# An encoder layer on one core: the seventh of eight input pairs by Strassen's products, weights split four blocks at a time, one pool of 8 KB raw tiles, and a first sum made by an adding DMA

## The chip, the core and the metric

The kernel runs on one core of a Trainium2 chip. The metric is the device time of one execution in microseconds (us). The core's engines are TensorE (PE, matrix products), VectorE (DVE), ScalarE (ACT), GpSimd (POOL) and SyncE (SP, which here only issues DMAs). They run side by side, each through its own queue in order, and wait for each other by semaphores.

## The reference

One layer of an encoder for 256 positions of 2048 channels, in float32: a feed-forward half-step, a mixer, and another feed-forward half-step.

```python
def _swiglu(x, w_gate, w_up, w_down):
    return (jax.nn.silu(x @ w_gate) * (x @ w_up)) @ w_down

def _macaron_ffn(x, pre_g, w_gate, w_up, w_down, post_g):
    return x + MACARON_WEIGHT * _rms_norm(_swiglu(_rms_norm(x, pre_g), w_gate, w_up, w_down), post_g)
...
    for l in range(DEPTH):
        h = _macaron_ffn(h, ffn1_pre_g[l], ffn1_w_gate[l], ffn1_w_up[l], ffn1_w_down[l], ffn1_post_g[l])
        h = _gated_mixers(h, mix_pre_g[l], w_in[l], b_gate[l], q_norm_g[l], k_norm_g[l],
                          w_attn_o[l], w_fourier[l], w_out[l], mix_post_g[l], rope)
        h = _macaron_ffn(h, ffn2_pre_g[l], ffn2_w_gate[l], ffn2_w_up[l], ffn2_w_down[l], ffn2_post_g[l])
```

The mixer is an attention branch (16 query heads, 4 key and value heads) and a Fourier branch, each behind a sigmoid gate. The hidden width of the feed-forward is 5632.

## The kernel before

**Products in pieces.** TensorE gets float32r operands. `split` (L104) cuts a float32 weight tile into a rounded part `hi` (ACT, L105) and the rest `lo` (DVE, L106), and `mm3` (L109) makes one product with three matmuls of 128x128 by 128x512 (L111, L112, L113): hi by hi, hi by lo, lo by hi. A block of weights below is 128 rows of 512 columns, 256 KB in DRAM, 2 KB in each partition. Every weight is read once from DRAM into a raw tile, split, and multiplied with both halves of the 256 positions.

**The feed-forward.** `ffn` (L714) works in 11 blocks of 512 hidden columns. The first two are multiplied plainly, column block by column block. For the nine others (f = 2 to 10) the products of the gate and up weights are made by `swiglu` (L562), and between them stand the products with the down weights, `row_line` (L666), two blocks behind. The 2048 input channels are eight pairs of 128-channel blocks. For six pairs (`BY_SEVEN`: 0, 1, 2, 4, 5, 6) the two halves of the positions, the two blocks of channels and the two weights (gate, up) make a 2x2 product of 2x2 blocks, done by Strassen's seven products instead of eight (`seven`, L606): 21 matmuls instead of 24. Pairs 3 and 7 are done plainly (`plain`, L576). The sums of the input that the seven products need are made once by `Forms` (L447) and kept split; the sums of the weights are made by DVE for each block of columns (`minus`, L586: four differences of one block of weights per pair), and so are the sums of the products at the end, with SiLU and the last multiplication (L591, L599, L603).

**The order of the work.** In this stage the order on DVE, ACT and PE is written out by hand (`manual_schedule`): each engine runs its instructions in the order of the program. The other queues (SP's and POOL's DMAs) are ordered by a scheduler. `Line` (L529) holds a queue of steps. A step has a part that makes weights ready (load, differences, split) and a part that uses them (matmuls, then sums or copies). `feed` (L535) puts a step in; while the queue is full it first runs `next`, which puts out the use of the oldest step; then it puts out the preparation of the new one. So DVE and ACT prepare up to eight steps ahead of the matmuls. `hold` on a step stops preparations after its use until a step without it has been used, so that sums of products stand ahead of further splits on DVE. A step holds two blocks of weights: two steps for each column block of `row_line`, four for a pair of seven products, the last with one block.

**Rooms.** Split tiles come from a ring: six pairs of 4 KB tiles, and two more 8 KB tiles out of `b8`, twelve rooms of 8 KB that also hold u (the input, split and transposed), the forms, y, h and other large tiles. Raw tiles come from five rooms of 4 KB, and for pairs 0, 2, 4 and 6 from `b8`, with one load of 1024 KB. `chunk` has three rooms of each of its two kinds. A room is given again when its last reader is done: a load waits for the split that read the room before, a split for the matmuls.

**The rows.** In `row_line` the first result is set into y. Later the first two column blocks are added to y by an adding DMA on POOL's queue (L706), the other two by copying y into PSUM ahead of the products (L690) and back (L700).

**Mixer.** It runs plain column blocks (`col_block`) and row blocks with two-block pieces of weights from the same rooms; `gate` (L1103) writes its sigmoids into `b8` rooms mB and zA; the fold of the Fourier branch adds by DMA while it loads (`load_f`, L934). `last_rows` (L265) ends each stage and starts the next.

## Time and profile before

| | |
|---|---|
| three timed runs | 1998.6, 1999.6 and 2001.35 us, median 1999.6 |
| the profiled execution | 2000.01 us, its span from the first to the last instruction 1997.9 us |
| granted TensorE clock | 0.998 |
| DMA | 434.19 MB, 217 GB/s on the mean |
| the span by engines | PE 99% busy, DVE 89%, ACT 65%, POOL 4% |

The shares of busy time and the chain that ended last are on the profile's page. A row of the windows gives, for a stretch of the span, the busy time and number of instructions of PE, PE's weight loads (PEld), DVE, ACT and POOL, then the granted clock, the share of the DMA engines and GB/s. A row of the groups by form gives the line, engine, operation, tiles and shapes, the number, then total busy time and mean ns of one, and behind the second bar the idle time ahead of them with what ended it. A row of the timeline gives start, duration and instruction. A row of the DMA issues gives the tile and source, the issuing queue, the number, the size of each, and the median us from issue to landing. The waits give who waited for whom: total us, times, longest.

### The profile page before, as it was taken

What the parts mean: (1) busy time and instruction counts of PE and PEld (TensorE: products, weight loads), DVE (VectorE), ACT (ScalarE), POOL (GpSimd) and SP (SyncE); (2) the same over time, 40 slices, a digit from 0 to 9 for tenths busy, and PEclk for the clock granted to TensorE, in tenths of its full rate; (3) what the DMA queues carried; (4) which work ended last, traced back from release to release, by engine and by line L of the source; (5) the groups of instructions that cost most, each with busy time, mean ns of one, the idle gap of its engine ahead of it and who ended that gap; (6) DMA issues with size and microseconds to landing.
All of it is one profiled execution on the core that took longest, in us unless ns stands there. A gap on an engine that the chain in (4) does not pass through costs nothing.

```text
span 1997.9 us, 25756 instructions
## 1 busy us (share of the span) xinstructions
PE 1983.4 (99%) x9146; PEld 1644.7 (82%) x9146; DVE 1776.0 (89%) x2306; ACT 1301.3 (65%) x1860; POOL 84.8 (4%) x94
## 2 busy tenths in 40 slices
PE   9999999999999999999999999999999999999998
PEld 7888888888888888888888888888888888888886
DVE  6999999999999878886877885878999999999996
ACT  7566766767666756556666564656667766677666
POOL 0000000000000010100000000000000000000002
PEclk9999999999999999999999999999999999999999
DMA  9657766677668796854555557565577766677673
GB/s 328 222 177 237 227 221 204 207 242 224 227 203 277 241 302 202 252 181 142 192 193 186 193 166 276 195 216 194 177 230 232 232 209 208 216 232 232 215 259 127
DMA packets 117584, 434.19 MB, mean 217 GB/s; under 512 B 12840, under 2 KB 18992, under 8 KB 106064
## 3 DMA queue, kind: packets, MB, share of 16 engines
q1 hardware_dynamic: 103888, 411.65, 60.4%
q0 software_dynamic: 13568, 20.91, 6.0%
q8 instruction: 71, 1.16, 0.2%
q14 instruction: 57, 0.47, 0.1%
HBM read 409.44 MB, written 6.29 MB: 208 GB/s over the span
## 4 chain that ended last, share of the span: by engine, by line
PE 98%; DVE 1%; DMA 1%; ACT 0%; issue 0%; SPq 0%; DVEq 0%; ACTq 0%
PE pc L112 20%; PE pc L111 20%; PE pc L113 20%; PE pr L113 11%; PE pr L112 11%; PE pr L111 11%; PE pt L184 2%; PE pe L111 0%; PE pe L113 0%; PE pf L112 0%; PE pf L111 0%; PE pf L113 0%; DVE wlo L106 0%; PE pe L112 0%; PE pt L1081 0%; DMA raw<-in_f_gate 0%
## 5 line engine op out<-in xcount | busy, mean ns | idle before, releaser
L106 DVE TENSOR_TENSOR wlo<-raw,whi 128x1024 fp32r<-128x1024 f32 (+1 forms) x567 | 680.7, 1219 | 96.2 <-ACT whi L105 94.1
L105 ACT ACTIVATE whi<-raw 128x1024 fp32r<-128x1024 f32 (+1 forms) x567 | 586.5, 1053 | 252.3 <-PE pc L113 96.1
L112 PE MATMUL pc<-wlo,fh 128*128 128x512 f32 x738 | 287.6, 390 | 0.0
L113 PE MATMUL pc<-whi,fl 128*128 128x512 f32 x738 | 287.6, 390 | 0.0
L111 PE MATMUL pc<-whi,fh 128*128 128x512 f32 x738 | 287.4, 389 | 0.0
L111 PE MATMUL pc<-whi,uh 128*128 128x512 f32 x688 | 271.6, 396 | 1.2 <-ACT uh L838 1.2
L113 PE MATMUL pc<-whi,ul 128*128 128x512 f32 x688 | 269.7, 392 | 0.0
L112 PE MATMUL pc<-wlo,uh 128*128 128x512 f32 x688 | 269.3, 392 | 0.1
L105 ACT ACTIVATE whi<-t 128x1024 fp32r<-128x1024 f32 (+1 forms) x198 | 171.5, 866 | 138.6 <-DVE t L586 133.6
L586 DVE TENSOR_TENSOR t<-raw 128x512 f32<-128x512 f32 (+1 forms) x252 | 208.9, 841 | 14.2 <-DMA raw<-in_f_gu 10.5
L111 PE MATMUL pr<-whi,hTh 128*128 128x512 f32 x544 | 213.6, 393 | 0.0
L113 PE MATMUL pr<-whi,hTl 128*128 128x512 f32 x544 | 212.0, 390 | 0.0
L112 PE MATMUL pr<-wlo,hTh 128*128 128x512 f32 x544 | 211.9, 390 | 0.0
L106 DVE TENSOR_TENSOR wlo<-t,whi 128x1024 fp32r<-128x1024 f32 (+1 forms) x198 | 193.4, 977 | 13.6 <-ACT whi L105 13.3
L105 ACT ACTIVATE w<-raw 128x1024 fp32r<-128x1024 f32 x144 | 151.9, 1055 | 40.4 <-DVE raw L586 35.2
L106 DVE TENSOR_TENSOR w<-raw,w 128x1024 fp32r<-128x1024 f32 x144 | 175.5, 1219 | 0.0
L112 PEld LDWEIGHTS pc<-wlo,fh 128*128 128x128 f32 x738 | 138.6, 188 | 29.1
L111 PEld LDWEIGHTS pc<-whi,fh 128*128 128x128 f32 x738 | 138.6, 188 | 29.0
L113 PEld LDWEIGHTS pc<-whi,fl 128*128 128x128 f32 x738 | 138.6, 188 | 28.8
L111 PEld LDWEIGHTS pc<-whi,uh 128*128 128x128 f32 x688 | 129.7, 188 | 27.9 <-ACT uh L838 2.7
L112 PEld LDWEIGHTS pc<-wlo,uh 128*128 128x128 f32 x688 | 129.6, 189 | 26.8 <-DVE wlo L106 1.7
L113 PEld LDWEIGHTS pc<-whi,ul 128*128 128x128 f32 x688 | 129.4, 188 | 27.0
(350 smaller groups left out, 3183.4 us busy)
## 6 DMA issues: line engine op xcount, KB each, us to landing
raw<-in_f_down SPq DMA_DIRECT2D x176, 512.0 KB, 5.2
raw<-in_f_gu SPq DMA_DIRECT2D x144, 512.0 KB, 4.5
raw<-in_f_gu SPq DMA_DIRECT2D x72, 1024.0 KB, 7.4
raw<-in_w_in SPq DMA_DIRECT2D x112, 512.0 KB, 4.4
raw<-in_f_up SPq DMA_DIRECT2D x32, 512.0 KB, 5.0
raw<-in_w_ao SPq DMA_DIRECT2D x32, 512.0 KB, 3.8
raw<-in_w_out SPq DMA_DIRECT2D x32, 512.0 KB, 4.9
raw<-in_f_gate SPq DMA_DIRECT2D x31, 512.0 KB, 5.8
```

The lines of the kernel that those rows point to most:

```text
L105: a = A.activation(hi, src, AF.Copy)
L106: v = V.tensor_tensor(out=lo, in0=src, in1=hi.bitcast(F32), op=ALU.subtract)
L111: T.matmul(ps, lh, rh, start=first, stop=False, skip_group_check=onto)
L112: T.matmul(ps, lh, rl, start=False, stop=False, skip_group_check=onto)
L113: return T.matmul(ps, ll, rh, start=False, stop=last, skip_group_check=onto)
L184: T.transpose(pt[:, j, :], src[:, j * P:(j + 1) * P], ident[:])
L586: V.tensor_tensor(out=out, in0=a, in1=b, op=ALU.subtract)
```

## The change

Seven pairs go through Strassen's products (`BY_SEVEN` is 0 to 6), and only pair 7 is plain. The seven products are formed in another way: a pair's four raw blocks are split at once and give four products (p1, g0, p5, u0); then three sums of blocks are split at once and give three (p6, p7, g1). The first sum is already in the raw tile: one block is loaded, the three others with a second load, and a third DMA, on POOL's queue with the operation add, adds a block of the weight onto the first (`Sums.fetch`). `Sums` keeps up to three pairs fetched (`SUMS_AHEAD`), across the end of a block of columns too. DVE makes one difference of one block and one of two blocks per pair, the second with a broadcast operand (`wide_ones`), put behind the split of the pair before. A pair's last three products are put behind the first four of the next pair (`late`).

`row_line` takes the four blocks of a column block as one step, with one load of 1024 KB. The ring is eight tiles of 8 KB, of which a step takes one for hi and one for lo: four steps (three while `more` is off). Plain pair 7 is loaded and split as one tile of four blocks, put in ahead of pair 6's last step; its up product of the second half goes onto p5 in PSUM, after x4 has been taken from p5.

Raw tiles are five rooms of 8 KB for everything. `b8` has eight rooms instead of twelve, `chunk` two instead of three (and one extra tile for the loads of the fold). The second half of u lives in two ring tiles; the gains, kT and vs in raw rooms; foT in `b8`; the sigmoids of the attention gates go to DRAM (`z_spill`) and are loaded back ahead of their use. The weights are packed on the host in the order that the new form needs (`_pairs`).

The core of the diff:

```diff
 RAW_BUFS = 5
-RING = 6
-RING_B8 = 2
-RAW_B8 = (0, 2, 4, 6)
-SPARE = (None, None, "chunk", "u")
+RING = 8
+SPARE = (None, None, "chunk", None)
 SPARE_NEXT = ("b8", None, None, None)
-B8 = 12
+B8 = 8
 PLAIN = 2
-BY_SEVEN = (0, 1, 2, 4, 5, 6)
-CH = 3
+BY_SEVEN = (0, 1, 2, 3, 4, 5, 6)
+SUMS_AHEAD = 2
+CH = 2
...
     def ring(src):
 
         n = src.shape[1]
-        i = turn["n"] = (turn["n"] + 1) % (RING + RING_B8)
-        if turn["more"] and i % 4 == 1:
-            both = big("w2", F32R, [P, 2, WP, NB])
-            hi, lo = both[:, 0], both[:, 1]
-        else:
-            hi = wring.tile([P, WP, NB], F32R, tag="hi", name="whi")
-            lo = wring.tile([P, WP, NB], F32R, tag="lo", name="wlo")
-        split(hi[:, 0:n, :], lo[:, 0:n, :], src)
+        hi, lo = (ring_room("w" + c, F32R, [P, CK, NB])[:, 0:n, :] for c in ("hi", "lo"))
+        split(hi, lo, src)
         return [(hi[:, i, :], lo[:, i, :]) for i in range(n)]
 
-    def raw_piece(src, i):
-        raw = wraw.tile([P, WP, NB], F32, tag="raw", name="raw")
-        load(raw[:], src.rearrange("p (i k c) -> p i k c", k=WP, c=NB)[:, i])
+    def wide(src):
+        raw = room("raw", F32, [P, CK, NB])
+        load(raw[:], src)
         return raw
...
-        def feed(self, ready, use, *then, hold=False):
-
-
-            while len(self.queue) >= RING + RING_B8 * turn["more"]:
+        def feed(self, ready, use, *then, hold=False, cost=1):
+
+
+            while sum(step[4] for step in self.queue) + cost > RING // 2 - (not turn["more"]):
                 self.next()
-            self.queue.append([ready, use, then, hold])
+            self.queue.append([ready, use, then, hold, cost])
...
+    class Sums:
+
+
+        def __init__(self, wgu, blocks):
+            self.todo = [(wgu[f], pair) for f in range(blocks) for pair in BY_SEVEN]
+            self.ready = []
+
+        def fetch(self):
+            w, pair = self.todo.pop(0)
+            src = w[pair // 2].rearrange("p (q k c) -> p q k c", q=2, c=NB)[:, pair % 2]
+            raw = room("raw", F32, [P, CK, NB])
+            load(raw[:, 0:1, :], src[:, 0:1])
+            load(raw[:, 1:CK, :], src[:, 1:CK])
+            nc.gpsimd.dma_start(raw[:, 0, :], src[:, 1], accum_op=ALU.add)
+            self.ready.append(raw)
+
+        def get(self):
+            while len(self.ready) <= SUMS_AHEAD and self.todo:
+                self.fetch()
+            return self.ready.pop(0)
...
+        def seven(pair, *then):
             a11, a12, na22, s1, s2, s3, s4 = forms.seven[pair]
             end = pair == BY_SEVEN[-1]
             h = {}
 
+            def products(ws):
+                for n, a, b in (("p1", a11, 1), ("g0", a12, 2), ("p5", s1, 0), ("u0", s4, 3)):
+                    mul(n, a, ws[b], end and n[0] == "p")
+
+            def sums_of(ws):
+                for n, a, b in (("p6", s2, 0), ("p7", s3, 1), ("g1", na22, 2)):
+                    mul(n, a, ws[b], end and n[0] == "p")
+
+            def wide_ones():
+                raw = h["raw"]
+                V.tensor_tensor(out=raw[:, 1:3, :], in0=raw[:, 0:1, :].to_broadcast([P, 2, NB]), in1=raw[:, 1:3, :],
+                                op=ALU.subtract)
+
             def first():
+                raw = h["raw"] = sums_.get()
+                ws = ring(raw[:])
+                V.tensor_tensor(out=raw[:, 0, :], in0=raw[:, 0, :], in1=raw[:, 3, :], op=ALU.subtract)
+                if not late:
+                    wide_ones()
+                return ws
+
+            line.feed(first, products, *then[0:1])
+            last = late.pop() if late else None
+            if last:
+                last(wide_ones)
+            late.append(lambda behind=None: line.feed(
+                lambda: (ring(h["raw"][:, 0:3, :]), behind and behind())[0], sums_of, *then[1:], hold=end))
...
+        late = []
+        sums = [copy, lambda: combine("x2", "p6", "x1", ALU.add), lambda: combine("x4", "p5", "x2", ALU.subtract),
+                lambda: combine("x3", "p7", "x2", ALU.add)]
+        gates = [lambda: combine("x1", "g0", "x1", ALU.add), lambda: combine("x2", "g1", "x3", ALU.add),
+                 lambda: silu(0), lambda: silu(1)]
+        ups = [lambda: combine("x4", "u0", "x4", ALU.add), lambda: times(0),
+               lambda: combine("x3", "p5", "x3", ALU.subtract), lambda: times(1)]
         for kg in range(KD // CK):
             a, b = 2 * kg, 2 * kg + 1
             if kg == KD // CK - 1:
+                seven(a, *sums)
                 if a in behind:
                     behind[a]()
+                four = {}
+
+                def plain_ones():
+                    src = w[b // 2].rearrange("p (q k c) -> p q k c", q=2, c=NB)[:, b % 2]
+                    four["w"] = ring(wide(src)[:])
+
+                line.feed(plain_ones, lambda ws: None, cost=0)
+                late.pop()()
+                line.feed(None, lambda: plain(b, 0, four["w"]), *gates, hold=True, cost=0)
+                line.feed(None, lambda: plain(b, 1, four["w"]), *ups)
...
-            for i in range(CK // WP):
-                line.feed(lambda i=i, cb=cb: ring(raw_piece(w[rb, cb], i)[:]),
-                          lambda b, cb=cb, i=i: use(b, cb, i),
-                          *([lambda t=t, cb=cb: out(t, cb) for t in range(NT)] if i == CK // WP - 1 else []))
+            line.feed(lambda cb=cb: ring(wide(w[rb, cb].rearrange("p (k c) -> p k c", k=CK))[:]),
+                      lambda b, cb=cb: use(b, cb), *[lambda t=t, cb=cb: out(t, cb) for t in range(NT)])
...
-        return tuple(big(f"u{c}{t}", F32R, [P, KD, P]) for c in "hl")
+        return tuple((ring_room if t else big)(f"u{c}{t}", F32R, [P, KD, P]) for c in "hl")
...
-        g = big(name)
+        g = room(name, F32, [P, D])
...
+            if dst is None:
+                A.activation(z[:], z[:], AF.Sigmoid)
+                load(cbs(z_spill[t], cb), z[:])
...
+    for t in range(NT):
+        zA.append(big(f"zA{t}"))
+        load(zA[t][:], z_spill[t])
```

More of the change, by code (lines that the diff above doesn't have):

```diff
@@ L552, in next @@
                 self.prepare()
-            _, use, then, self.held = self.queue.pop(0)
+            _, use, then, self.held, _ = self.queue.pop(0)
             use()
@@ L571, in mul @@
             begun.add(n)
-        def raw(pair, i):
-            return raw_piece(w[pair // 2], pair % 2 * 2 + i)
-        def plain(pair, i, *then, hold=False):
-            def use(b):
-                for t in range(NT):
-                    for j in range(2):
-                        k = 2 * pair + j
-                        mul("gu"[i] + str(t), forms.plain[k][t], b[j], k == KD - 1)
-            line.feed(lambda: ring(raw(pair, i)[:]), use, *then, hold=hold)
-        def minus(out, a, b):
-            V.tensor_tensor(out=out, in0=a, in1=b, op=ALU.subtract)
@@ L627, in second @@
-            def second():
-                b = ring(h["t"][:])
-                minus(h["t"][:, 0, :], h["ra"][:, 1, :], h["rb"][:, 1, :])
-                return b
-            def two(n, a, m, b, last):
-                def use(ws):
-                    mul(n, a, ws[0], last)
-                    mul(m, b, ws[1], last)
-                return use
-            line.feed(first, two("u0", s4, "g0", a12, False))
-            line.feed(second, two("p5", s1, "p7", s3, end), hold=end)
-            if between:
-                between()
@@ L642, in seven @@
-            line.feed(lambda: ring(h["ra"][:]), two("p1", a11, "p6", s2, end), *then[0:2], hold=end)
-            line.feed(lambda: ring(h["t"][:, 0:1, :]), lambda ws: mul("g1", na22, ws[0]), *then[2:], hold=end)
-        sums = [copy, lambda: add("x2", "p6", "x1"), lambda: add("x3", "p7", "x2"), lambda: add("x2", "p5", "x2"),
-                lambda: add("x5", "p5", "x3")]
-        gates = [lambda: add("x1", "g0", "x1"), lambda: add("x3", "g1", "x3"), lambda: silu(0), lambda: silu(1)]
-        ups = [lambda: add("x2", "u0", "x2"), lambda: times(0), lambda: add("x5", "u1", "x5"), lambda: times(1)]
+            def products(ws):
+                for n, a, b in (("p1", a11, 1), ("g0", a12, 2), ("p5", s1, 0), ("u0", s4, 3)):
+                    mul(n, a, ws[b], end and n[0] == "p")
@@ L661, in swiglu @@
                     behind[b]()
-            else:
-                seven(a, lambda: plain(b, 0))
-                plain(b, 1)
     def row_line(line, ch, w, rb, y, way, ahead):
         first = way == "set"
-        rooms = {(0, 0): (ptr, "tr"), (1, 0): (ptr, "tr"), (1, 1): (ptr, "tr")} if not first else {}
+        rooms = {(0, 0): (ptr, "tr"), (1, 0): (ptr, "tr")} if not first else {}
         ps = {}
@@ L898, in norm_rope @@
         return o
[L900 to L902 removed]
+    dps, dcs, odd, first, alt = (four[n] for n in ("dps", "dcs", "odd", "first", "alt"))
+    mm_ = xpool.tile([NYR, 3 * P + 2 * NYR], F32R, tag="xt", name="mid")
+    mid, mids = mm_[0:NS, 0:2 * P + 2 * NYR], mm_[:, 2 * P + 2 * NYR:]
+    mraw = work("mraw", [NS, 2 * P + 2 * NYR])
+    load(mraw[:], dft_mid)
+    kT, vs = [], []
     ueo = [[big(f"u{n}{c}", F32R, [P, KD, P]) for c in "hl"] for n in "eo"]
@@ L951, in fold_f @@
                                    op0=ALU.mult, op1=ALU.add)
-        hi = wring.tile([P, 2, NB], F32R, tag="hi", name="whi")
-        lo = wring.tile([P, 2, NB], F32R, tag="lo", name="wlo")
-        split(hi[:], lo[:], raw[:])
+        both = ring_room("w", F32R, [P, 2, 2, NB])
+        hi, lo = both[:, 0], both[:, 1]
+        split(hi, lo, raw[:])
         e, o = slice(0, EW), slice(EW, NB)
@@ L1129, in fourier_weights @@
                                    op0=ALU.mult, op1=ALU.add)
-            hi = wring.tile([P, 2, NB], F32R, tag="hi", name="whi")
-            lo = wring.tile([P, 2, NB], F32R, tag="lo", name="wlo")
-            split(hi[:], lo[:], raw[:])
+            both = ring_room("w", F32R, [P, 2, 2, NB])
+            hi, lo = both[:, 0], both[:, 1]
+            split(hi, lo, raw[:])
             forms.append((hi, lo))
```

152 lines of the change are left out of this document (76 added, 76 removed).

## The prediction

> **What bounds the kernel now.** I read the page's engine shares and its chain first, then the windows, the timeline, the groups by form, the DMA issues and the waits.
>
> ```profile
> span 1997.9 us, 25756 instructions
> PE 1983.4 (99%) x9146; PEld 1644.7 (82%) x9146; DVE 1776.0 (89%) x2306; ACT 1301.3 (65%) x1860; POOL 84.8 (4%) x94
> PE 98%; DVE 1%; DMA 1%; ACT 0%; issue 0%; SPq 0%; DVEq 0%; ACTq 0%
> ```
>
> TensorE (PE) is the chain, and only 14.5 us of the span have no matmul. So whatever takes matmuls away can shorten the kernel, and whatever makes PE wait lengthens it at once. The change is inside the feed-forward line, so the next rows are one block of it.
>
> ```profile
> 236.61 0.87 PE pt L184 x8
> ...
> 298.83 0.87 PE pt L184 x8
> ```
>
> ```profile
> 236.61:298.83 62.22, 62.22 (x280) 51.53 (x279) 60.09 (x69) 42.17 (x54) 3.23 (x5) 1.00 0.69 218
> 720.00:900.00 180.00, 177.17 (x900) 150.58 (x899) 146.85 (x216) 103.60 (x160) 13.08 (x12) 0.99 0.72 222
> ```
>
> ```profile
> 240.51 0.39 PE L113 MATMUL pr<-whi,hTl 128*128 128x512 f32 x1
> ...
> 242.55 0.39 PE L113 MATMUL pr<-whi,hTl 128*128 128x512 f32 x1
> ```
>
> From one group of transposes to the next is one block: 62.22 us, PE busy throughout, and VectorE (DVE, the third engine of the window row) busy for 60.09 of them, 97%. DVE is a second bound just below the first. A block has 96 matmuls in the row line (4 column blocks x 2 row halves x 4 k x 3) and 6 x 21 + 2 x 24 = 174 in the eight pairs: 270, and 8 transposes at 0.87 us. One matmul therefore costs (62.22 - 0.87) / 270 = 0.2272 us of PE, not the 0.39 that its row says: nine steps from 240.51 to 242.55 are 0.227 each, and the records overlap.
>
> **Matmuls removed.** Pair 3 had 24 matmuls and gets 21, in 9 blocks of 2 feed-forwards: 54 x 0.2272 = 12.3 us, 0.68 per block. All of it is on the path. A block without waits would be 61.54 us.
>
> **DVE's work.** Prices by form:
>
> ```profile
> L106 DVE TENSOR_TENSOR wlo<-raw,whi 128x1024 fp32r<-128x1024 f32 x565 | 679.3, 1220 | 91.9 <-ACT whi L105 89.8
> L586 DVE TENSOR_TENSOR t<-raw 128x512 f32<-128x512 f32 x180 | 121.1, 689 | 3.7
> L105 ACT ACTIVATE whi<-t 128x1024 fp32r<-128x1024 f32 x108 | 114.8, 1063 | 93.7 <-DVE t L586 90.3 <-PE pc L113 2.7
> L105 ACT ACTIVATE whi<-t 128x512 fp32r<-128x512 f32 x90 | 56.8, 631 | 45.0 <-DVE t L586 43.4 <-PE pc L113 1.6
> L700 ACT ACTIVATE y<-pr 128x512 f32<-128x512 f32 x44 | 24.8, 596 | 8.1 <-PE pr L113 8.0
> ```
>
> ```profile
> 274.13 2.36 DVE L106 TENSOR_TENSOR wlo<-raw,whi 128x1024 fp32r<-128x1024 f32 x2
> 276.41 1.22 DVE L106 TENSOR_TENSOR w<-raw,w 128x1024 fp32r<-128x1024 f32 x1
> 277.54 2.35 DVE L106 TENSOR_TENSOR wlo<-raw,whi 128x1024 fp32r<-128x1024 f32 x2
> 279.82 4.53 DVE L591 TENSOR_TENSOR x<-pc,x 128x512 f32<-128x512 f32 x7
> ```
>
> Call 512 columns a part. One part takes 0.689 us and two 1.220: 0.535 per part and 0.15 fixed. Two in a row take 2.36, not 2.44, so in a row only 0.07 of the fixed cost is left. Four parts last 2.29 and hold DVE for 2.21; three hold it 1.68, two 1.14, one 0.61. No DVE row of four parts is there: it lies between 4 x 0.535 = 2.14 and two rows of two parts, 2.36, and I take the middle one, which the slope gives. ScalarE (ACT) likewise: 1.93 for four parts, 1.49 for three.
>
> Before, a block gives DVE 102 parts in 68 instructions (66 split, 24 differences, 10 sums, 2 transposed); after, 101 in 44 (7 x 10 for the pairs, 4 plain, 16 rows, 9 sums, 2). That saves 0.535 + 24 x 0.07 = 2.2 us a block: DVE in total fits below 61.54.
>
> But the total does not decide; the order does. A pair now costs DVE a split of four parts, one difference, a split of three, and a difference of two parts: 2.21 + 0.61 + 1.68 + 1.14 = 5.63 us. PE uses a pair in 21 x 0.2272 = 4.77. So in the seven pairs PE gains 0.86 us per pair on DVE, and lives on the lead made while the rows ran. Before, it was worse per pair (11 parts), but plain pair 3 in the middle let DVE catch up, and eight steps of two parts stood ahead. The ring now holds four steps (eight tiles of 8 KB, hi and lo). When the last row matmul ends (t = 0), DVE has ready the four-part steps of pairs 0 and 1 and the three-part step of pair 0: 33 matmuls, 7.50 us of PE. Pair 2 needs the ring room that the row step just left: ACT's copy of y 0.60, its split 1.93, DVE's 2.29: ready at 4.82. From there DVE runs without pause: pair 6 is ready at 4.82 + 4 x 5.63 = 27.34, PE would be there at 7.50 + 4 x 4.77 = 26.58: **0.76 late**. The three-part step of pair 6 stands behind a difference (0.61), pair 5's three parts (1.68), a difference of two (1.14) and the whole plain split (2.21): 27.34 + 5.64 + 1.68 = 34.66, where PE arrives at 27.34 + 4.77 = 32.11: **2.55 late**. These 3.3 us are the floor, with every load on time; with no fixed cost at all (13 parts from pair 6's first split to its last: 6.96) it would still be 1.8.
>
> That splits really stand ahead of the sums is seen above: five splits run, then the seven sums. The same in the code after: the plain tile and the first two row tiles are split ahead of the sums that free p5, since only pair 6's last step holds the queue back.
>
> **Loads.** Five raw rooms of 8 KB; two hold the next block's first pairs, fetched ahead. A new load starts when a room comes free:
>
> ```profile
> SPq L86 <- DVE wlo L106: 968.1, 433, 8.9
> ```
>
> ```profile
> raw<-in_f_gu SPq DMA_DIRECT2D x144, 512.0 KB, 4.5
> raw<-in_f_gu SPq DMA_DIRECT2D x72, 1024.0 KB, 7.4
> y<-part POOLq DMA_DIRECT2D x32, 256.0 KB, 7.9
> fraw<-in_w_f POOLq DMA_DIRECT2D x16, 252.0 KB, 7.2
> h<-h_spill SPq DMA_DIRECT2D x4, 1024.0 KB, 4.8
> raw<-in_f_gate SPq DMA_DIRECT2D x2, 256.0 KB, 4.4
> ```
>
> SP's DMA queue waited 433 times for DVE's split to free a room; that stays. 1024 KB lands in 7.4 us behind another load in this stage, in 4.8 where little else runs.
>
> The plain tile (rooms: pairs 5, 6, two fetched ahead, and this) starts when pair 4's three-part split ends, at 27.34 - 2.29 - 1.14 = 24.0 (rounded). It lands after L1, ACT takes 1.93, DVE 2.29, and pair 6's last split follows: 24.0 + L1 + 5.9 = 29.9 + L1 instead of 34.66, so it decides from L1 = 4.8 up. Two loads of its neighbour and an adding DMA run beside it, so I take 7.4: 37.3, **5.2 late** in place of 2.55.
>
> The second row tile gets the room that the plain split frees, at 28.2 + L1. It lands after L2, then 1.93 + 2.29, and the two sums that free p5, 0.61 + 0.69: 33.7 + L1 + L2. PE needs p5 after pair 6's last 9 matmuls and 18 plain ones, 6.13 us. With L1 = 7.4 and L2 = 4.8 (only the first row tile is near it): 45.9 against 37.3 + 6.1 = 43.4, **2.5 late**.
>
> What queues behind these waits: DVE's stalled split holds back the sums, ACT's its copies out of PSUM, and PE waits for both; the rows then have 21.8 us of PE against 4 x 2.21 of DVE, so DVE's lead is full again at the next block, and the loss recurs.
>
> Together 0.8 + 5.2 + 2.5 = 8.5 us a block; with 4.8 for both loads 5.9, with 7.4 for both 11.1.
>
> **The adding DMA.** 126 of 256 KB, 33 MB.
>
> ```profile
> q1 hardware_dynamic: 103888, 411.65, 60.4%
> q0 software_dynamic: 13568, 20.91, 6.0%
> ```
>
> ```profile
> L706 POOL DMA_DIRECT2D y<-part x32 | 28.1, 1014 | 582.1 <-ACT part L705 582.1
> ```
>
> At q0's price, 6.0% for 20.91 MB, that is 9.5% of the DMA engines' time beside 66%: no bound. One sum takes 4.4 for its first block, 1.0 of POOL, 7.9 to land: 13.3 us. From the room's release to its split DVE has 4 x 1.14 + 3 x 4.5 = 18.0, less ACT's 1.93: 16.1, so it is hidden by 2.8. On POOL it stands behind adds of y, which wait for row matmuls some 20 us earlier; behind it stand only later adds, whose y is read a block later. I take 0; up to 2 us a block if it lands late.
>
> **The rest.** Where rooms move (u in the ring, kT and vs in raw rooms, 8 tiles for 12, two chunks for three), and gates go to DRAM and back (eight stores of 256 KB, two loads a row block ahead of use, on SP), the mixing stage has cover: PE's idle in 720 to 900 is 2.8 us. Losing that is the gain's end; the other is two spills of h laid bare:
>
> ```profile
> h_spill<-h SPq DMA_DIRECT2D x4, 1024.0 KB, 7.2
> ```
>
> So -3 to +14; I take +3, nearer to the idle now. Four-part row steps change no matmul count.
>
> **The sum.** 18 x 8.5 = 153, -12.3, +3: +144. Against the profiled execution (span 1997.9, 2000.0 in all) that is 2144; the median of the runs is 0.4 lower: **2143 us**. Its own range: 18 x 5.9 - 12.3 = +94, to 18 x 11.1 - 12.3 + 14 = +202: 2094 to 2201.
>
> **Rivals.**
>
> Faster: DVE keeps the lead, and only the matmuls go: 1999.6 - 12.3 = 1987. For it: DVE has 2.2 us less per block, in fewer instructions. It decides if a pair costs DVE no more than 4.77 + 2.68 / 4 = 5.4 us and the plain split does not stand ahead. Against it: ten parts at 0.535 are 5.35 before any fixed cost. Chance 0.11. A rule of the Trainium skill speaks for this rival: Perfetto Trace Analysis, Optimizing Scalar/DVE Operations, gives DVE an overhead of about 60 ns per instruction on SBUF and advises "Grouping and performing larger operations" where the engine is saturated. The trace agrees on the size (0.07 in a row); by the rule the block falls by 0.68 us, by the rows' order it grows.
>
> Only DVE's order costs, since loads land in 4.7 or less: 18 x 3.3 - 12.3 = +47, 2047. For it: 512 KB lands in 4.5. Against it: twice the bytes, an added queue. Chance 0.15.
>
> Adds land late as well, 2 us more a block: 2143 + 36 = 2179, within the likeliest case's range and chance.
>
> No change: the waits eat just the 0.68 us a block, 2000; no mechanism gives this. Chance 0.03.
>
> **How the numbers follow.** The likeliest has 0.68, the floor case 0.15, faster 0.11, no change 0.03, above 2205 0.03. The range 2040 to 2205 leaves out the last three. About 0.2% is what a measurement of this kernel can tell from no change. Faster 0.11, same 0.03, slower 0.86.
>
> **What would show it.** Right: PE no longer full in the block windows, the block near 69 to 70 us; waits of PE's matmuls for wlo and the sums at each block's end; DVE idle behind ACT's split, ACT behind a load of the plain tile; DVE rows near 2.29 and 1.75 us. Wrong: blocks of 61.5 us with PE full; or waits in the mixing stage instead; or splits waiting for the adding DMA in mid-block.

## The result and the profile after

The changed kernel takes 2162.7 us (median of 4 runs, 2160.8 to 2168.7) against 1999.7 us of the kernel before on the same chip: a ratio of 1.082, 95% interval 1.0803 to 1.0836. The forecast was 2143 us in a range of 2040 to 2205.

The profiled execution of the kernel after took 2168.7 us, the slowest of the four; the steps below are counted in it. These are the page's first lines and its chain that ended last:

```profile
span 2166.5 us, 25126 instructions
PE 2042.1 (94%) x9092; PEld 1657.6 (77%) x9092; DVE 1746.2 (81%) x1880; ACT 1288.3 (59%) x1556; POOL 194.6 (9%) x220
PE 61%; DVE 18%; issue 8%; DMA 8%; ACT 4%; DVEq 0%; SPq 0%; ACTq 0%
```

Before, PE was 98% of the chain; now it is 61%, and DVE and DMA have taken most of the rest. DVE's own work did fall (1776.0 to 1746.2 us), so it isn't a sum of work that grew. The same three stretches of both kernels, cut at the transposes that open the first feed-forward line, the mixing stage and the second line and at those that close it, show where the time went (windows; columns as in the section on the profile). The kernel before:

```profile
111.97:672.03 560.06, 560.06 (x2503) 463.81 (x2502) 543.45 (x615) 380.88 (x478) 28.05 (x32) 1.00 0.69 223
672.03:1400.40 728.37, 725.24 (x3517) 604.85 (x3516) 579.35 (x882) 443.45 (x740) 17.47 (x16) 1.00 0.63 208
1400.40:1960.46 560.06, 560.06 (x2503) 463.87 (x2502) 543.24 (x615) 380.30 (x478) 27.99 (x32) 1.00 0.69 221
```

The kernel after:

```profile
111.89:748.33 636.44, 585.34 (x2477) 468.64 (x2476) 530.94 (x404) 374.58 (x327) 79.40 (x91) 0.96 0.76 223
748.33:1495.89 747.56, 733.70 (x3517) 608.27 (x3516) 578.10 (x880) 443.83 (x740) 19.84 (x19) 0.99 0.63 207
1495.89:2129.08 633.19, 585.04 (x2476) 468.57 (x2475) 529.73 (x403) 373.31 (x325) 79.36 (x91) 0.96 0.77 221
```

The two lines lost 76.4 and 73.1 us, the mixing stage 19.2; what lies ahead of and behind these stretches is the same. A line holds nine blocks: 62.23 us each before, 70.5 on average after (69.7 to 72.4; only the last block of the second line takes 66.1). With 0.68 us of matmuls taken away, a block without waits would be 61.5, so 9.0 us of each block are new. One block, from its transposes on, and the end of its eight pairs in three parts (windows of the kernel after):

```profile
254.91:324.81 69.90, 64.59 (x277) 51.76 (x276) 58.49 (x45) 41.63 (x36) 9.62 (x11) 0.98 0.77 221
293.66:298.20 4.54, 0.89 (x3) 0.19 (x1) 3.96 (x2) 4.07 (x4) 0.00 (x0) 1.00 0.68 226
298.20:301.90 3.70, 3.70 (x9) 2.91 (x10) 2.29 (x1) 0.76 (x2) 0.00 (x0) 0.55 0.93 392
301.90:306.00 4.10, 4.10 (x18) 3.03 (x16) 2.73 (x2) 1.34 (x1) 0.00 (x0) 0.99 0.94 382
```

In the first part PE waits. In the second it is busy throughout, but nine matmuls take as long as eighteen do in the third: the granted clock is 0.55. PE's timeline at these places:

```profile
293.66 0.39 PE L119 MATMUL pc<-whi,fl 128*128 128x512 f32 x1
295.57 0.50 PE L117 MATMUL pc<-whi,fh 128*128 128x512 f32 x1 [1.53 <-ACT whi L111]
298.20 0.52 PE L118 MATMUL pc<-wlo,fh 128*128 128x512 f32 x1 [2.12 <-DVE wlo L112]
299.37 0.63 PE L118 MATMUL pc<-wlo,fh 128*128 128x512 f32 x1
299.80 0.63 PE L119 MATMUL pc<-whi,fl 128*128 128x512 f32 x1
305.67 0.40 PE L119 MATMUL pc<-whi,frest 128*128 128x512 f32 x1
306.95 0.50 PE L117 MATMUL pc<-whi,frest 128*128 128x512 f32 x1 [0.88 <-DVE x L610]
```

From start to start, with 0.227 taken off for each matmul, the last step of pair 6 is 1.68 + 2.40 = 4.1 us late. Then the steps are 0.43 in place of 0.227 (1.7 in all), and the matmul onto p5 waits for the sums that free it, 1.28 - 0.23 = 1.05. Pair 6's first step, at 288.15, had cost 0.84. Together that is 7.7 of this block's 8.4; some tenths at single starts are the rest.

Why it is late stands in ACT's and DVE's timelines of the same block. First ACT's:

```profile
292.24 3.29 ACT L111 ACTIVATE whi<-raw 128x2048 fp32r<-128x2048 f32 x2 [3.67 <-DMA raw<-in_f_gu]
301.33 1.92 ACT L111 ACTIVATE whi<-raw 128x2048 fp32r<-128x2048 f32 x1 [2.94 <-PE pc L118]
```

Then DVE's:

```profile
294.19 3.96 DVE L112 TENSOR_TENSOR wlo<-raw,whi 128x2048 fp32r<-128x2048 f32 x2 [1.49 <-ACT whi L111]
303.27 2.29 DVE L112 TENSOR_TENSOR wlo<-raw,whi 128x2048 fp32r<-128x2048 f32 x1 [2.56 <-PE pc L119]
305.48 3.80 DVE L610 TENSOR_TENSOR x<-pc,x 128x512 f32<-128x512 f32 x6
```

ACT waits 3.67 us for the plain tile's load; both splits behind it (the plain tile's and pair 6's last, grouped in one row as x2) come late, and DVE idles 1.49 us in front of them. Then a row tile's split, whose part on ACT waited 2.94 us for PE to free a ring room, stands ahead of the six sums. This last wait differs between blocks: by ACT's timeline it is for the row tile's load in 14 of the 18 blocks, for a ring room in three, this block among them. The prices, by groups of forms, and the plain tile's load, from the DMA issues:

```profile
L112 DVE TENSOR_TENSOR wlo<-raw,whi 128x2048 fp32r<-128x2048 f32 x224 | 510.8, 2288 | 167.1 <-ACT whi L111 161.5 <-PE pc L119 4.2 <-PE pc L118 1.2
L112 DVE TENSOR_TENSOR wlo<-raw,whi 128x1536 fp32r<-128x1536 f32 x126 | 220.8, 1752 | 32.9 <-ACT whi L111 32.9
```

```profile
raw<-in_f_gu SPq DMA_DIRECT2D x18, 1024.0 KB, 6.9
```

### The profile page after: what moved, and what is told of

It reads as the page before. It is cut to its first block, busy times and chain, and to the rows that moved or that the text cites. A ratio compares the mean times of both kernels' runs of the same rounds, so it can differ in the third digit from the quotient of the medians.

```text
span 2166.5 us, 25126 instructions
## 1 busy us (share of the span) xinstructions
PE 2042.1 (94%) x9092; PEld 1657.6 (77%) x9092; DVE 1746.2 (81%) x1880; ACT 1288.3 (59%) x1556; POOL 194.6 (9%) x220
## 3 DMA queue, kind: packets, MB, share of 16 engines
q1 hardware_dynamic: 101584, 415.85, 55.8%
q0 software_dynamic: 31712, 53.95, 15.3%
## 4 chain that ended last, share of the span: by engine, by line
PE 61%; DVE 18%; issue 8%; DMA 8%; ACT 4%; DVEq 0%; SPq 0%; ACTq 0%
DVE wlo L112 10%; PE pr L117 10%; PE pr L119 10%; PE pr L118 10%; PE pc L118 9%; PE pc L117 9%; PE pc L119 9%; DMA raw<-in_f_gu 5%; DVE raw L640 3%; ACT whi L111 2%; DMA raw<-in_f_down 2%; PE pt L195 2%; DVE w L112 1%; DVE x L610 1%; ACT w L111 1%
## 5 line engine op out<-in xcount | busy, mean ns | idle before, releaser
L112 DVE TENSOR_TENSOR wlo<-raw,whi 128x2048 fp32r<-128x2048 f32 (+1 forms) x353 | 732.9, 2088 | 204.0 <-ACT whi L111 198.4
L111 ACT ACTIVATE whi<-raw 128x2048 fp32r<-128x2048 f32 (+1 forms) x353 | 611.1, 1751 | 328.3 <-DVE raw L640 152.5
L118 PE MATMUL pc<-wlo,fh 128*128 128x512 f32 x864 | 354.2, 410 | 50.2 <-DVE wlo L112 48.7
L112 DVE TENSOR_TENSOR w<-raw,w 128x1024 fp32r<-128x1024 f32 (+1 forms) x266 | 320.7, 1217 | 86.1 <-ACT w L111 82.5
L117 PE MATMUL pc<-whi,fh 128*128 128x512 f32 x864 | 346.8, 401 | 39.7 <-ACT whi L111 38.8
L111 ACT ACTIVATE w<-raw 128x1024 fp32r<-128x1024 f32 (+1 forms) x266 | 277.5, 1055 | 159.5 <-PE pc L119 73.6
L117 PE MATMUL pc<-w,uh 128*128 128x512 f32 x688 | 273.8, 399 | 7.4 <-ACT w L111 6.4
L118 PE MATMUL pc<-w,uh 128*128 128x512 f32 x688 | 271.8, 395 | 1.6 <-DVE w L112 1.6
L119 PE MATMUL pc<-w,ul 128*128 128x512 f32 x688 | 271.3, 394 | 0.0
L117 PEld LDWEIGHTS pc<-w,uh 128*128 128x128 f32 x688 | 130.6, 190 | 35.8 <-ACT w L111 7.3
L640 DVE TENSOR_TENSOR raw<-raw 128x1024 f32<-128x1024 f32 x126 | 153.6, 1219 | 0.6
L118 PEld LDWEIGHTS pc<-w,uh 128*128 128x128 f32 x688 | 130.9, 190 | 29.8 <-DVE w L112 4.4
L119 PEld LDWEIGHTS pc<-w,ul 128*128 128x128 f32 x688 | 130.8, 190 | 27.4
L117 PEld LDWEIGHTS pr<-whi,hTh 128*128 128x128 f32 x648 | 121.7, 188 | 26.0 <-DVE y L722 0.8
```

What stands on the lines that cost most here:

```text
L111: a = A.activation(hi, src, AF.Copy)
L112: v = V.tensor_tensor(out=lo, in0=src, in1=hi.bitcast(F32), op=ALU.subtract)
L117: T.matmul(ps, lh, rh, start=first, stop=False, skip_group_check=onto)
L118: T.matmul(ps, lh, rl, start=False, stop=False, skip_group_check=onto)
L119: return T.matmul(ps, ll, rh, start=False, stop=last, skip_group_check=onto)
L640: V.tensor_tensor(out=raw[:, 1:3, :], in0=raw[:, 0:1, :].to_broadcast([P, 2, NB]), in1=raw[:, 1:3, :], op=ALU.subtract)
```

## The experiments

Theory: at the end of each block PE waits for DVE's order of work (a floor of some 3.3 us) and for two late loads, because the raw rooms are taken by sums fetched ahead. Rivals: the adding DMA; the stretch at half clock; DVE's sum of work; the new rooms. All edits are to the kernel after unless said otherwise, and "SUMS_AHEAD 1" ("AHEAD 1" in the table) is the first run's kernel. Times are medians, with the ratio to the kernel before and its 95% interval.

| run | us | ratio (95%) | block, us | mixing stage, us |
|---|---|---|---|---|
| before | 1999.7 | 1 | 62.2 | 728.4 |
| after | 2162.7 | 1.082 (1.0803 to 1.0836) | 69.7 to 72.4 | 747.6 |
| SUMS_AHEAD 1 | 2093.2 | 1.0464 (1.0447 to 1.0481) | 65.6 or 67.1 | 745.8 |
| six raw rooms | 2088.5 | 1.0447 (1.0432 to 1.0463) | 65.6 or 67.2 | 744.8 |
| no adding DMA | 2138.2 | 1.0699 (1.068 to 1.0717) | 68.3 to 70.3 | 746.8 |
| matmuls in the wait | 2177.8 | 1.088 (1.0861 to 1.0899) | 69.1 to 74.7 | 745.0 |
| before, seventh pair alone | 2060.7 | 1.0306 (1.0289 to 1.0323) | 65.5 | 727.2 |
| AHEAD 1, no double difference | 2027.4 | 1.0137 (1.0117 to 1.0156) | 61.6 to 63.4 | 744.7 |
| AHEAD 1, splits in halves | 2071.9 | 1.0359 (1.0342 to 1.0376) | 64.8 or 65.8 | 744.8 |
| AHEAD 1, ten ring rooms, four raw | 2266.8 | 1.1333 (1.1311 to 1.1355) | 71.8 to 75.4 | 779.0 |
| AHEAD 1, difference on GpSimd | 2213.8 | 1.1068 (1.1051 to 1.1084) | 72.3 to 74.4 | 745.2 |
| nine ring rooms | 2167.4 | 1.0836 (1.0814 to 1.0858) | 69.3 to 72.5 | 748.0 |
| AHEAD 1, a room per piece | 2113.3 | 1.0567 (1.0551 to 1.0583) | 65.6 or 67.2 | 763.9 |
| AHEAD 1, values' copies moved back | 2087.0 | 1.0436 (1.0418 to 1.0453) | 65.6 or 67.1 | 738.5 |

The column of blocks gives their usual lengths; the first and last block of a line can lie outside.

**Fewer sums ahead.**

```diff
-SUMS_AHEAD = 2
+SUMS_AHEAD = 1
```

> One pair fewer is fetched ahead (SUMS_AHEAD 1 for 2), so one raw room more is free at a block's end. Theory (late loads of the plain and row tiles behind rooms that are held): the plain tile and the second row tile load earlier by about a pair of DVE's work (5.6 us), the wait of pair 6's last step falls to the 2.5 us that DVE's order makes, the wait for p5 goes; block 66 to 68 us for 70.6, time 2080 to 2115. Rival (the adding DMA is what comes late): with less fetched ahead the pairs' splits wait longer, slower than 2163. Rival (DVE's order alone): 2163 as it is.

Measured: 2093.2 us, and a block of 65.57 us on PE's timeline waits at these three places and hardly elsewhere:

```profile
279.10 0.50 PE L118 MATMUL pc<-wlo,fh 128*128 128x512 f32 x1 [0.67 <-DVE wlo L112]
284.23 0.50 PE L117 MATMUL pc<-whi,fh 128*128 128x512 f32 x1 [0.30 <-ACT whi L111]
286.50 0.50 PE L118 MATMUL pc<-wlo,fh 128*128 128x512 f32 x1 [1.76 <-DVE wlo L112]
```

From the starts ahead of them, less 0.227 a matmul, that is 0.83 us for pair 6's first step and 2.5 for its last: the floor that the prediction worked out, 0.76 and 2.55, and no wait for p5. ACT's waits for the two loads, in the kernel after:

```profile
ACT whi L111 <- DMA raw<-in_f_gu: 72.2, 16, 6.0
ACT whi L111 <- DMA raw<-in_f_down: 50.2, 21, 3.7
```

And here:

```profile
ACT whi L111 <- DMA raw<-in_f_gu: 4.9, 1, 4.9
ACT whi L111 <- DMA raw<-in_f_down: 3.5, 1, 3.5
```

Two fetched pairs that hold raw rooms past the end of the block make the loads late.

**Six raw rooms**, with SUMS_AHEAD at 2 as in the kernel after. The room is paid with two work tiles and the fold's fifth chunk.

```diff
-RAW_BUFS = 5
+RAW_BUFS = 6
...
-F_AHEAD = 4
+F_AHEAD = 3
...
-    chunk5 = pool("chunk5", 1)
-    wk = pool("wk", 8)
+    wk = pool("wk", 6)
...
```

> Six raw rooms of 8 KB for five; the space comes from two work tiles and the extra tile of the fold, whose loads then run three ahead for four. Theory: as with one pair fewer ahead, but the fetch keeps its lead: block about 66 us, and the mixing stage, where two raw rooms hold kT and vs, gives back a good part of its 19 us: 2060 to 2095. Rival (DVE's order alone): blocks as they are, 2145 to 2163. Rival (rooms of the ring, not of raw tiles): no change.

Measured: 2088.5 us, and blocks of the same two lengths as with SUMS_AHEAD 1. So it is the free rooms, not what is fetched ahead, that count. The mixing stage got only 2.7 us back, against the expectation.

**No adding DMA.** The first sum lacks one of its blocks.

```diff
-            nc.gpsimd.dma_start(raw[:, 0, :], src[:, 1], accum_op=ALU.add)
```

> The adding DMA of the first sum is left out (the first sum then lacks one block of the weight). Theory: it is hidden, and the DMA engines are no bound: 2163 within 10 us. Rival (the adding DMA, its issues on GpSimd or its traffic make the waits): the time falls by most of the 163 us.

Measured: 2138.2 us, 24.5 below the kernel after, where the theory expected none; its issues and PE's waits there:

```profile
raw<-in_f_gu SPq DMA_DIRECT2D x18, 1024.0 KB, 4.9
```

```profile
PE pc L117 <- DVE x L609: 23.5, 17, 2.5
PE pc L117 <- ACT whi L111: 5.6, 18, 0.8
```

And in the kernel after:

```profile
PE pc L117 <- ACT whi L111: 38.8, 18, 3.9
PE pc L117 <- DVE x L610: 8.6, 12, 1.2
```

The plain tile lands in 4.9 in place of 6.9 us, and the waits for ACT's split go (38.8 to 5.6). But the waits for the sums that free p5 take part of it back (8.6 to 23.5). The adding DMA costs 1.4 us a block, through its neighbour's load and not by being late itself: no split waits for it in mid-block. That is more than the 0 taken, and within the bound of 2.

**Matmuls in the wait.** Is the stretch at half clock a cost of its own?

```diff
+WARM_MMS = 14
...
+                if pair == BY_SEVEN[-2]:
+                    for _ in range(WARM_MMS):
+                        T.matmul(ps["g1"][:], na22[0], ws[2][0], start=False, stop=False)
```

> The kernel after, with 14 more matmuls behind the first products of pair 5's second step, onto the second gate tile (so the gate's second half isn't the reference's); they lie where TensorE waits for pair 6's second step in every block. Theory: in that wait TensorE has 0.89 us of work in 4.54, and the matmuls behind it then run at 0.427 us in place of 0.227 for some 3.7 us; with 14 x 0.227 = 3.2 us of work in the wait the rows at 0.427 go, and a block is shorter by up to 1.8 us: 2163 - 18 x 1.8 = 2130 us, and mean granted clock from 0.972 to 0.985 or more. Rival: the stretch at half speed only covers a wait for VectorE's combinations that ends at the same time anyway: the clock rises, the time stays at 2155 to 2165 us and the wait for x grows by what the stretch loses. Second rival: the wait was shorter than the 3.2 us of added work, and the time rises.

Measured: 2177.8 us. The stretch behind the first wait is gone in all but three blocks and the mean clock rises from 0.972 to 0.984, but no time is gained. PE's timeline of one block:

```profile
300.52 0.50 PE L119 MATMUL pc<-wlo,fh 128*128 128x512 f32 x1 [2.12 <-DVE wlo L113]
309.31 0.80 PE L118 MATMUL pc<-whi,frest 128*128 128x512 f32 x1 [2.51 <-DVE x L611]
309.90 0.63 PE L119 MATMUL pc<-wlo,frest 128*128 128x512 f32 x1
310.33 0.63 PE L120 MATMUL pc<-whi,frest 128*128 128x512 f32 x1
```

Full speed only brings PE sooner to the sums, where it now waits 2.5 us in place of 0.9 (the waits for x grow from 8.6 to 40.1 us in all), and in ten of the 18 blocks half clock follows there. The first rival holds in its mechanism: in the kernel after the slow matmuls cover a wait. The time itself came out 13 us above what that rival gave. A likely reason is that the slow matmuls now follow the last wait of the block, where they cover nothing; this isn't separated from the added matmuls that find no wait to fill. In this block the row tile's split waits for its load (ACT, 3.56 us), as the prediction had it.

**The seventh pair alone**: the kernel before, with pair 3 through the seven products in the old form, and two small constants of the Fourier part in other rooms.

```diff
-BY_SEVEN = (0, 1, 2, 4, 5, 6)
+BY_SEVEN = (0, 1, 2, 3, 4, 5, 6)
...
```

> The kernel before with pair 3 as a seventh pair in the old form, nothing else of the change (two small tiles moved to make room for the forms). Theory (DVE bounds the block): DVE gets 109 parts in 74 instructions, 109 x 0.535 + 74 x 0.07 = 63.5 us, more than PE's 61.5, and the last pairs come late on top: block 63.5 to 66, time 2023 to 2065. Rival (PE alone bounds, the loss is due to the new pieces and rooms): 1987.

Measured: 2060.7 us. A window of one block's length:

```profile
240.00:305.54 65.54, 63.59 (x277) 50.21 (x276) 64.29 (x75) 43.75 (x56) 3.06 (x4) 1.00 0.65 205
```

DVE is busy for 64.29 of 65.54 us: here its sum of work is the bound. The new form with loads on time has the same 65.57 us with DVE busy for 58.3, so there the sum isn't. The new form of the seven products has thus gained nothing in the blocks over the old one, even with its loads on time.

**Without the double difference** (`wide_ones`, the difference of two blocks at once), on SUMS_AHEAD 1.

```diff
             def wide_ones():
                 raw = h["raw"]
-                V.tensor_tensor(out=raw[:, 1:3, :], in0=raw[:, 0:1, :].to_broadcast([P, 2, NB]), in1=raw[:, 1:3, :],
-                                op=ALU.subtract)
+                pass
```

> The kernel after with SUMS_AHEAD 1 and without the subtraction of two blocks at once (the 128x1024 row of 1.22 us, seven to a block); two of the seven products of each pair so take raw blocks in place of sums, and the output isn't the reference's. Theory (VectorE's order bounds the block once the loads are on time): a pair costs VectorE 2.29 + 1.75 + 0.69 = 4.73 us in place of 5.95, beside 21 matmuls of 0.2272 = 4.77 us, the waits for wlo at the end of a block go, and blocks fall from 65.57 and 67.14 to between 61.0 and 62.5: 2093 - 18 x (4 to 5.3) = 1998 to 2021 us. Rival (late loads and ScalarE's splits set the end of the block): blocks stay at 65 or more and the time at 2080 to 2093 us.

Measured: 2027.4 us, 6 above the expected span: the first block of the first line and the last of each stay long, and of those between, 61.6 to 63.4, seven are above the 62.5 expected. One of the longer:

```profile
240.73:304.09 63.36, 61.83 (x276) 50.88 (x275) 50.77 (x38) 41.99 (x36) 11.68 (x14) 1.00 0.85 247
```

With 4.73 us of DVE a pair, PE keeps its lead and the floor goes: four blocks take 61.6 us, the length without waits. In the block shown PE waits once, 1.5 us for the sums that free p5. The profiled execution is 31 us longer than that of the kernel before; 16 of these are the mixing stage and 15 the two lines.

**Splits in halves**, on SUMS_AHEAD 1: more instructions, less delay.

```diff
-        split(hi, lo, src)
+        for i in range(0, n, WP):
+            part = slice(i, min(i + WP, n))
+            split(hi[:, part, :], lo[:, part, :], src[:, part, :])
```

> The kernel after with SUMS_AHEAD 1, and each split of four or three blocks written as two instructions of two blocks (or two and one) on each engine, so that VectorE can start when ScalarE has half, and TensorE when VectorE has half. Price: 2 x 1.22 = 2.44 us in place of 2.29 on VectorE and 2 x 1.06 = 2.12 in place of 1.91 on ScalarE, eleven splits of four blocks and seven of three, about 2.7 us of VectorE in a block. Theory A (the waits are for the end of one long split: 0.67 and 1.76 us for wlo at a block's end): the waits shrink by 0.8 to 1.2 us each, blocks 64 to 65.3 us, 2050 to 2085 us. Theory B (VectorE's work in the bunched stretch sets it): the dearer splits add to the wait, 65.6 to 68 us, 2093 to 2130 us.

Measured: 2071.9 us, as theory A has it. A block of it:

```profile
242.39:307.15 64.76, 62.39 (x276) 50.79 (x275) 58.89 (x63) 43.09 (x55) 10.57 (x13) 1.00 0.82 242
```

DVE has 0.6 us more work than with SUMS_AHEAD 1 (58.31 in a block of 65.57), and the block is 0.8 shorter: not the sum decides, but when a split ends. The Trainium skill (Perfetto Trace Analysis, Optimizing Scalar/DVE Operations) says that where these engines aren't saturated but cause bubbles elsewhere, breaking up instructions may complete work sooner; the trace agrees. The advice of the Trainium skill in the same section to group, weighed in the prediction, is for an engine that is saturated, as DVE nearly was in the kernel before (97%).

**A longer lead**, on SUMS_AHEAD 1: ten ring rooms, four raw rooms.

```diff
-RAW_BUFS = 5
-RING = 8
+RAW_BUFS = 4
+RING = 10
...
```

> The kernel after with SUMS_AHEAD 1, ten rooms in the ring (five splits ahead in place of four), four raw rooms, two work tiles fewer and without the fifth Fourier chunk. With SUMS_AHEAD 1 alone a block is 65.57 or 67.14 us and VectorE is busy for 58.5 of it: it has some 7 us idle, yet TensorE waits for its splits at the end of a block. Theory A (VectorE's place in the order, not its sum of work, sets the block: it idles behind the ring's rooms and is late where its work is bunched): with one split more ahead it uses part of the idle time, and blocks fall to 62 to 64 us. Theory B (its sum of work sets it): 65 to 66 us. Rival (four raw rooms make the loads late again): 68 us or more, and waits for ScalarE's splits behind a load. The mixing stage has two raw rooms to itself in place of three and may get longer, 746 to 780 us; the time goes by both: A 2030 to 2085, B 2085 to 2125.

Measured: 2266.8 us. The waits on PE:

```profile
PE pc L116 <- DVE x L609: 100.1, 18, 9.6
```

The rival came true: with four raw rooms the row tile is later still, and its split stands ahead of the sums in every block (5.6 us each). Whether a longer lead alone would do, this run can't say: its rooms are paid for with the loads.

**The double difference on GpSimd**, on SUMS_AHEAD 1.

```diff
-                V.tensor_tensor(out=raw[:, 1:3, :], in0=raw[:, 0:1, :].to_broadcast([P, 2, NB]), in1=raw[:, 1:3, :],
-                                op=ALU.subtract)
+                nc.gpsimd.tensor_tensor(out=raw[:, 1:3, :], in0=raw[:, 0:1, :].to_broadcast([P, 2, NB]), in1=raw[:, 1:3, :],
+                                        op=ALU.subtract)
```

> The kernel after with SUMS_AHEAD 1 and the subtraction of two blocks at once on GpSimd in place of VectorE. GpSimd's product of 128x512 takes 1.37 us in the trace of before, so one of 128x1024 some 2.7 us, an estimate, and seven 19 us of a block. Theory (VectorE's order bounds the block): VectorE loses 7 x 1.22 us, as where the subtraction is left out, the later start of the second split costs little because it has a whole step of slack, and the time comes to 2000 to 2040 us. Rival: the two engines hinder each other, VectorE's rows of 2.29 and 1.75 us grow by what GpSimd takes (up to 19 us in a block of 65), and the time is 2093 us or more. The Trainium skill (Perfetto Trace Analysis, Optimizing Scalar/DVE Operations) says that the two share a read port and that moving work between them might not help; by it the rival would be the likelier.

Measured: 2213.8 us. Groups by form:

```profile
L640 POOL TENSOR_TENSOR raw<-raw 128x1024 f32<-128x1024 f32 x126 | 436.9, 3468 | 145.9 <-DVE raw L646 66.7 <-issue 51.5 <-DMA raw<-in_f_down 21.1
L112 DVE TENSOR_TENSOR wlo<-raw,whi 128x2048 fp32r<-128x2048 f32 x224 | 708.6, 3177 | 101.3 <-ACT whi L111 99.2 <-PE pc L119 1.7
```

The rival holds. DVE's split of four parts grows from 2.29 to 3.18 us on the mean, and GpSimd's subtraction takes 3.47: 198 us more of DVE for these rows alone than in the kernel after, where 154 were taken away. The mean holds splits with nothing beside them, which still take 2.29. In mid-block, beside GpSimd, the splits of four and three parts in a row take 6.15 us, against 4.03 in the run without the subtraction, and DVE has no pause between them; so it is these longer splits, and not GpSimd's later result, that make the pair long there. The trace agrees with the rule of the Trainium skill named in the expectation.

**The mixing stage: the ring.** Nine rooms, paid as the sixth raw room was.

```diff
-RING = 8
+RING = 9
...
```

> The kernel after with nine rooms in the ring in place of eight (paid with two work tiles and the fifth Fourier chunk, as in the run with six raw rooms, but five raw rooms here). Theory on the mixing stage: two of the ring's rooms hold the second token half's input there, so its splits have six; with seven, the waits for split weights shrink and the stage falls from 747.6 to 728 to 738 us, the blocks staying at 69.7 to 72.4: 2145 to 2160 us. Rival: the stage's loss isn't from the ring, it stays at 743 to 749 us. For the blocks: if the wait of the ring's next tile for TensorE (2.94 us ahead of the last split of a block) sets them, they fall by 1 us or more, 2145 us or less; if the late loads do, they stay.

Measured: 2167.4 us, stage 748.0. Its waits for the sums:

```profile
PE pc L116 <- DVE x L609: 12.2, 13, 2.7
```

Neither the stage nor the blocks gain from a ring room, and PE's wait for the sums stays (8.6 and 12.2 us in all). ACT's splits in the lines hardly wait for a ring room any more (50.2 us in all in the kernel after, 10.8 here), but they wait for the row tiles' loads instead (50.2 and 61.2). So the late load is the bound, and where a ring room came last in the kernel after, the load must have been close behind it. Since the price is that of the run with six raw rooms, that run's gain came from the raw room.

**The mixing stage: a room per piece**, on SUMS_AHEAD 1.

```diff
-            if "raw" not in whole:
-                whole["raw"] = room("raw", F32, [P, CK, NB])
-            raw = whole["raw"][:, ks, :]
+            raw = room("raw", F32, [P, CK, NB])[:, 0:WP, :]
```

> The kernel after with SUMS_AHEAD 1, and outside the hand-written lines each piece of 512 KB has a raw room of its own (half of it used) in place of two pieces sharing one. Theory on the mixing stage's 17 to 19 us: a shared room comes free only when both halves are split, so loads restart in pairs and the splits run dry; with rooms of their own the stage falls from 745.8 to 730 to 740 us. Rival: the order in which ScalarE is given its work there (the next weights' split behind the copies of the values, which wait for TensorE) sets the stage: 743 to 748 us. Second rival: with half of each room unused fewer bytes are ahead, and the stage gets longer, 750 us or more. The blocks of the two lines stay at 65.6 and 67.1 us in all cases: 2075 to 2087 us by the theory, 2090 to 2100 by the rivals.

Measured: 2113.3 us, stage 763.9: the second rival. Sharing a room isn't the loss, and with fewer bytes ahead the stage gets longer. The time is 13 us above what the rivals gave.

**The mixing stage: the order on ScalarE**, on SUMS_AHEAD 1. In the kernel after, ACT's timeline at the end of the values' products:

```profile
808.43 1.06 ACT L111 ACTIVATE w<-raw 128x1024 fp32r<-128x1024 f32 x1 [1.66 <-PE pc L119]
818.35 0.60 ACT L111 ACTIVATE ueh<-pt 128x512 fp32r<-128x512 f32 x1 [8.85 <-PE pt L935]
...
824.92 0.69 ACT L1194 ACTIVATE vt<-pc,r0r 128x512 f32<-128x512 f32 x1 [4.45 <-PE pc L119]
...
828.49 1.04 ACT L111 ACTIVATE w<-raw 128x1024 fp32r<-128x1024 f32 x1
```

No weights are split for 19 us; the next split comes behind the values' copies, which wait for PE. The kernel before has the same lines in the same order, but there the first copy waits for 0.93 us, and the next split follows at 751.60:

```profile
748.63 0.69 ACT L1167 ACTIVATE vt<-pc,r0r 128x512 f32<-128x512 f32 x1 [0.93 <-PE pc L113]
```

The edit puts these copies behind the start of the next gate:

```diff
-    for t in range(NT):
-        vt = work("vt")
+    def values_out():
+        for t in range(NT):
+            vt = work("vt")
...
-    gate(10, mB, 0, between=[lambda b=b: fold_tokens(b) for b in range(1, 4)]
+    gate(10, mB, 0, between=[values_out] + [lambda b=b: fold_tokens(b) for b in range(1, 4)]
```

> The kernel after with SUMS_AHEAD 1, and in the mixing stage the copies and splits of the values (vt, vs) put in program order behind the start of the next gate's products in place of ahead of them. With SUMS_AHEAD 1 alone, TensorE waits at the end of the values' products 4.2 and 2.0 us, and then runs eight matmuls at 0.427 us: together some 8 us, of the stage's 745.8 against 728.4 in the kernel before. Theory (order): ScalarE has nothing to do for 4.4 us and stands at vt, which waits for TensorE, with the next weights' split behind it; moved back, the split is done in time, the three rows go and the stage falls to 736 to 740 us, the time from 2093 to 2083 to 2088 us. Rival (rooms): the next split waits for a raw room or a ring room that is still in use, whatever the order: the wait for w stays at 4 us and the time at 2090 to 2097 us.

Measured: 2087.0 us, stage 738.5, as the theory of the order has it. PE's waits for split weights, with SUMS_AHEAD 1 alone and then with the copies moved:

```profile
PE pc L117 <- ACT w L111: 5.8, 2, 4.0
```

```profile
PE pc L117 <- ACT w L111: 2.2, 1, 2.2
```

So 7 of the stage's 17 us hang on an order on ACT in which the copies come ahead of the next split. The order itself isn't new, so the change must have made it costly; by which of the moved rooms isn't shown. The other 10 stay open: no raw room, ring room or sharing that was tried gives them back.

No version here beats the kernel before, and of the new form's versions that leave nothing out none beats the old form with the seventh pair, 2060.7. Halves with six raw rooms and the moved copies together weren't tried; taking off the single gains, 4.7 for the rooms, 21.3 for the halves and 6.2 for the copies, from SUMS_AHEAD 1 gives 2061 us, an estimate, still slower than the kernel before.

## Why the prediction was right, step by step

- **Matmuls removed, 12.3 us.** As predicted: 26 or 27 fewer records in each line, and block lengths add up with 61.5 as the base.
- **DVE's prices.** 2.29 and 1.75 us for four and three parts were forecast; 2288 and 1752 ns are measured.
- **The floor of 3.3 us a block.** Shown by SUMS_AHEAD 1: 0.83 and 2.5 against 0.76 and 2.55. It is there with both remedies for the loads. DVE's pair takes 5.73 us from split to split there, 5.63 predicted. The rival built on the floor, 2047 us, still was too low for them, 2093 and 2088. Of the 46 us missing with SUMS_AHEAD 1, some 17 are the stage, 9 the 1.6 us that half clock adds to six blocks, 6 the last block of the first line, where two gains are loaded into raw rooms and the plain tile's load is late once more, and the rest some 0.7 us in every block that no term held.
- **Late loads.** The mechanism was right: ACT behind the plain tile's load, DVE idle behind ACT, the sums behind a row tile's split. Pair 6's last step is 4.1 late in place of 5.2, the load 6.9 us in place of the 7.4 taken. The wait for p5 is 1.05 in place of 2.5, and 2.5 where PE arrives there at full clock. In 14 of the 18 blocks the split that holds the sums back waits for the second load, as the prediction named it; in three, the block shown among them, for a ring room, and a ninth ring room changes nothing.
- **Half clock** was missing from the sum: 1.8 us a block of it. It stands in the place of the rest of the wait for p5, as the added matmuls show; the two together are 2.8 against the 2.5 predicted. So the sum of one block held, 7.7 against 8.5, for a reason that was in part another. Where PE still waits for p5, the sums that free it set the end whatever the clock does before; in the six blocks without that wait, one of them the last of all, it is luck that half clock is of the wait's size. On average a block lost 9.0, since many are longer than the one laid out here.
- **The adding DMA.** Taken as hidden, cost 1.4 us a block by slowing a neighbour's load. The 7.4 us taken for that load was chosen with the adding DMA beside it, so the sum held this cost in another term.
- **The mixing stage is the mis-sized term**: +3 taken, bound +14, +19.2 measured. The step argued from the stage's idle time and from gates sent to DRAM. The runs showed 7 us of it in ScalarE's order of instructions, which the prediction didn't look at; some 10 stay open.
- **The total**: +144 forecast, +168.6 in the profiled execution, +163 in the medians. Of the 24.6 missing in the profiled one, 16 are the mixing stage and 9 the blocks.
- **The rivals.** Faster at 1987 fell on DVE's order, as argued against it: a pair at 5.7 us of DVE beside 4.77 of PE. Where a pair was cut to 4.73, the floor was gone.

## What to carry to other kernels

An engine with idle time in a stage can still set its end: ask when its last piece must be ready, and lay out its order against the matmuls from the last moment at which it had a full lead. A buffer that holds something early is one that a later load doesn't have; fetching further ahead with the same rooms made each block some 4 us longer. And where rooms are moved out of a tight stage, price the stage that gets them too, its order on each engine included.

## What the runs showed of the hardware

TensorE's clock can fall behind short waits. After 4.5 us with 0.89 us of work, nine matmuls take 3.7 us, 0.43 each for most of them in place of 0.227, at a granted clock of 0.55. Where matmuls filled that gap, one wait of 2.5 us was followed by seven at 0.43; in four blocks of that run waits of much the same length were not. The same waits in neighbouring blocks with SUMS_AHEAD 1 (2.95 us with 0.89 of work) are followed by the slow stretch in six and not in most others, which makes the two lengths 65.57 and 67.14. The Trainium skill (TensorE: Matmul & The Clock Gate, What's actually happening) has a free-running window of about 3.4 us that decides between full and half clock. The two block lengths and the stretch of 3.7 us fit that. That an idle window of 3.4 us is needed doesn't agree: 2.5 us were enough.

GpSimd hinders VectorE: beside a subtraction of 128x1024 on GpSimd, VectorE's two splits of a pair, with both operands in SBUF, take 6.15 us in a row in place of 4.03.

A byte on the queue of the adding DMAs takes about twice the DMA engines' time: 15.3% for 53.95 MB, against 55.8% for 415.85 MB on the other queue, by the page of the kernel after. The packets there are also smaller, 1.7 KB on the mean against 4.1 (31712 and 101584 packets); which of the two makes the price isn't shown.
